# Where the second layer's norm is applied, and where its Gram products are issued: a two-layer trunk of gated attention and RWKV-7 in fp32

## The chip, the core and the metric

The kernel runs on one core of one Trainium2 chip. The metric is the device time of one execution in microseconds. Five engines work beside each other, each through its own queue in order: TensorE (PE, its weight loads shown as PEld), VectorE (DVE), ScalarE (ACT), GpSimd (POOL) and SyncE (SP, which issues DMAs).

## What is computed

T = 512 tokens of D = 2048 channels go through two residual layers. The first is a gated differential attention with 8 heads, the second a gated RWKV-7 time mixing with 32 heads of 64 channels. Each layer is `x + W_out(mixer(RMSNorm(x)) * silu(gate))`. What the change touches is the second layer's start:

```
h = rms_norm(x, gain)                       # x * rsqrt(mean(x*x) + eps) * gain, per token
p = h @ w_in                                # r, k, v, g (2048 columns each), dw, da (96 each)
p = p + (token_shift(p) - p) * mu           # token_shift: the row of the token before, zero for the first
r, k, v, g, dw, da = split(p)
w_log = -softplus(-(w0 + tanh(dw) @ decay_up)) - 0.5
a = sigmoid(a0 + da @ iclr_up)
...
S = S * w_t + sa * b_t + v_t * k_t          # a 64 x 64 state per head, token after token
y = S @ r_t
```

After this come a group norm over each head, a bonus term, the gate and the output projection with the residual.

## The kernel before, in words

**Number format.** All matmuls of the projections work on fp32 numbers split into a high and a low fp32r part. One product is three matmuls, high x high, high x low, low x high (`mm3`, L106, matmul on L108). Weights come by DMA from SP's queue (`load_w`, L78); `split_w` makes the high part wh on ACT (L96) and the low part wl on DVE (L97), with two buffers of each. The input h is kept transposed, channels on partitions, as 16 tiles hH and 16 tiles hL of 128 x 512 (`make_h`, L561: ACT writes hH on L567, DVE writes hL on L568, both from a PSUM tile that the transposes of PE filled).

**Layer 0** runs its eight heads one after the other. A head's attention is a `Chain`: a generator whose steps are issued by `tick` (L139) behind a set number of the next head's projection matmuls, so that PE's order is written out by hand. Its output projection goes over four blocks of 512 columns (loop `cb`, L537). For each, 192 matmuls fill four PSUM tiles (one per 128 tokens, number t), DVE adds the residual input (L549), ACT stores the sum x1 to memory (L550) and sums its squares into ssx (L552); then PE transposes the 16 squares of 128 x 128 (L556), four into one PSUM tile, and `make_h` writes the tiles of h with the gain but without the norm.

**The passage.** Layer 1 opens its own pools, sets its masks (POOL), sums ssx (L1009), takes the reciprocal root on DVE (`rsqrt`, L63 to L70, integer start and three Newton steps), spreads each token's factor over 128 columns (`rep`, L1016), transposes it (L1017) and copies it to `rb` (L1019): a 128 x 512 tile that holds every token's factor on every partition. The first projection is the pair dw, da ("dwda": two times 96 columns, 96 matmuls). `unit_chan` runs a group of four channel blocks for dw, then the same four for da.

**Mixing.** `shift_mix` takes a projection from PSUM. DVE multiplies it by rb into `pmix`, which has a zero column in front (L606); ACT scales it by 1 - mu (L607); DVE adds mu times the same tile shifted by one token (L608).

**Layer 1's pairs.** Sixteen pairs of heads, j = 0 to 15, each with 128 channels: projections k, r, v (48 matmuls each), and from j = 3 on also the gate of pair j - 3. Behind k comes `stage1` (decay, the tiles AR and BK; AR's first half on L724, its sums' split on L579), behind r comes `stage2`: AR's second half (L744), the Gram products gp on PE (32 products of 64 or 128 columns, L755), their masking into G on DVE (L762), and stores that hand them to `t_solve`. `t_solve` (L790) inverts the triangular matrices on DVE with 62 small operations (L810, L812) and stores Tm to memory (td, L814). `t_combine` (L820) reads it back as TT (DMAs on SP, L826), transposes on DVE (T, L834), and multiplies with G on PE twice (px, L840 and L847). `scan_pair` (L905) then carries the state over eight chunks of 64 tokens, three small products each (L916, L927, L934) with copies on ACT (L919, L929), state updates on DVE (VS, L938/L941) and copies on POOL (SA, L922). `outputs` issues the products Y (L956, and with SA on L960), `centre` takes the mean off (L971 to L973: s, yc). The steps of t_combine, scan_pair and outputs of pair j - 1 form the chain that `tick` issues behind the matmuls of pair j, at set distances (GAP_D = 18, GAP_X = 27, GAP_T = 8, then 5 or 4 matmuls).

**What sets the order.** Each engine's queue is filled at build time by a list scheduler that works from priorities (`high_priority`, with the offsets AHEAD, SCAN and SOLVE) and from anchors (`issue_after`: not before a given matmul in PE's order). On the chip each queue runs in that order.

Of the kernel before, what the change touches and what calls it, by code (L numbers as in the profile page):

```python
# [13 lines left out]
F32 = mybir.dt.float32  # L14
# [3 lines left out]
AF = mybir.ActivationFunctionType  # L18
ALU = mybir.AluOpType
AX = mybir.AxisListType  # L20
# [3 lines left out]
P = 128  # L24
D = 2048
T = 512
KT = D // P
NT = T // P
NH = 8
EPS = 1e-6  # L30
# [8 lines left out]
AHEAD, SCAN, SOLVE = 2000, 3000, 4000  # L39
# [74 lines left out]
class Chain:  # L114
# [23 lines left out]

def tick(g, m, at):  # L139

    if g.chains:
# [157 lines left out]
def head_vg(g, h, vg):  # L299

    nc, w = g.nc, g.work
    V = w.tile([P, NT, 256], F32R, name="V", tag="V", bufs=1)
    VL = w.tile([P, NT, 256], F32R, name="VL", tag="VL", bufs=1)
    G = w.tile([P, NT, 256], F32, name="G", tag="G", bufs=2)
# [12 lines left out]

def attention(g, h, qkT, qkL, sq, V, VL, G, gap, rows=None):


    nc, w = g.nc, g.work
    yT = w.tile([P, 2, T], F32, name="yTh", tag="yTh", bufs=2)
    blocks = [Ctx() for _ in range(NT)]

    def scores(t):
# [105 lines left out]
def layer0(g, aps):  # L431
# [71 lines left out]
    with ExitStack() as cx:  # L503
# [29 lines left out]

        yH, yL = Rows(rows, 0), Rows(rows, 1)
        g.ssx = g.const.tile([P, NT, 4], F32, name="ssx")
        g.hH, g.hL = [], []
        for cb in range(4):  # L537
            cs = slice(cb * 512, (cb + 1) * 512)
            pts = unit_tok(g, yH, yL, [(aps["da_w_out"][0], cb * 512, 512)], 512, more=all_rows)
            if cb < 2:  # L540
                xq = g.work.tile([P, NT, 512], F32, name="xq", tag="qkT", bufs=2)
                xs = [xq[:, t, :] for t in range(NT)]
            else:
                tags, nb = (("t1",), 4) if cb == 2 else (("p0", "p1"), 2)
                xs = [g.work.tile([P, 512], F32, name="xr", tag=tags[t % len(tags)], bufs=nb)[:] for t in range(NT)]
            for t in range(NT):
                xr = xs[t]
                nc.sync.dma_start(out=xr, in_=aps["x"][0, t * P : (t + 1) * P, cs])
                nc.vector.tensor_add(xr, xr, pts[t][:])  # L549
                nc.scalar.dma_start(out=g.xd[t * P : (t + 1) * P, cs], in_=xr)  # L550
                junk = g.work.tile([P, 512], F32, name="junkx", tag="a", bufs=2)
                nc.scalar.activation(junk[:], xr, AF.Square, accum_out=g.ssx[:, t, cb : cb + 1])  # L552
            for k in range(4):
                ps = g.ps.tile([P, 512], F32, name="pt", tag="pb")
                for t in range(NT):
                    nc.tensor.transpose(ps[:, t * P : (t + 1) * P], xs[t][:, k * P : (k + 1) * P], g.ident[:])  # L556
                make_h(g, ps, KT + cb * 4 + k)
    lx.close()


def make_h(g, ps, col):  # L561

    nc = g.nc
    hh = g.hp.tile([P, T], F32R, name="hH", tag="hH")
    hl = g.hp.tile([P, T], F32R, name="hL", tag="hL")
    w = g.prm_a[:, col : col + 1]
    m = nc.scalar.activation(hh[:], ps[:], AF.Copy, scale=w)  # L567
    nc.vector.scalar_tensor_tensor(hl[:], ps[:], w, hh[:].bitcast(F32), ALU.mult, ALU.subtract)  # L568
    g.hH.append(hh)
    g.hL.append(hl)  # L570
    return m.ins
# [8 lines left out]
    return hh, hl  # L580


def unit_chan(g, parts, cols, step=P):

    nc = g.nc
    n = cols // step
    pts = [g.pp.tile([P, 512], F32, name="pp", tag="pp") for _ in range(n)]
    KG = 8 if cols == P else 4
    for k0 in range(0, KT, KG):
        wh, wl = split_w(g, parts, KG, cols, k0)  # L590
        for c in range(n):
            s = slice(c * step, (c + 1) * step)
            for k in range(KG):
                kk = k0 + k
                mm3(nc, pts[c][:step, :], wh[:, k, s], wl[:, k, s], g.hH[kk][:], g.hL[kk][:],
                    kk == 0, kk == KT - 1, g, 3 * kk)
    return pts


@urgent  # L600
def shift_mix(g, ps, rows, mu, omu, tag, bufs=2):

    nc, w = g.nc, g.work
    p_ = g.pmix
    o_ = w.tile([P, T], F32, name="mix" + tag, tag=tag, bufs=bufs)
    nc.vector.tensor_mul(p_[:rows, 1:], ps[:rows, :], g.rb[:rows, :])  # L606
    nc.scalar.activation(o_[:rows, :], p_[:rows, 1:], AF.Copy, scale=omu)  # L607
    nc.vector.scalar_tensor_tensor(o_[:rows, :], p_[:rows, 0:T], mu, o_[:rows, :], ALU.mult, ALU.add)  # L608
    return o_


C = 64
# [3 lines left out]
RK = 96  # L616
# [30 lines left out]
def rwkv_masks(g):  # L647
# [8 lines left out]
    for lo in (0, C):  # L656
# [5 lines left out]
    g.pmix = c.tile([P, T + 1], F32, name="pmix")  # L662
    nc.gpsimd.memset(g.pmix[:, 0:1], 0.0)
# [73 lines left out]
    return p  # L737


def stage2(g, j, r, p, before):  # L740

    nc, w, BK = g.nc, g.work, p.BK
    col = lambda n: g.prm[n][:, j : j + 1]
    nc.vector.tensor_mul(p.AR[:, :, 1, :], r[:].rearrange("p (c t) -> p c t", c=NC_), p.E[:, :, 1:])  # L744
    nc.vector.scalar_tensor_tensor(r[:], r[:], col("hrk"), p.f[:], ALU.mult, ALU.mult)
    p.rf = r
    p.G = w.tile([P, NC_, 2, 2, C], F32, name="G1", tag="G1", bufs=2)
    p.BKT = w.tile([P, NC_, P], F32, name="BKT", tag="BKT", bufs=2)
    halves = []
# [64 lines left out]
    nc.sync.dma_start(out=g.td[j % 2].rearrange("q l t -> l q t"), in_=Tm[:])  # L814


GAP_D, GAP_X, GAP_T = 18, 27, 8


def t_combine(g, j, p):  # L820
# [20 lines left out]
                             start=True, stop=True, tile_position=(b0, b0 + HALF))  # L841
    for _, _, _, hi in blocks:
        nc.scalar.copy(X[hi], px[hi, :N].rearrange("p (c s) -> p c s", c=NC_))
    yield GAP_X, None
    for h, b0, lo, hi in blocks:
        for c in range(NC_):
# [1 line left out]
                             start=True, stop=True, tile_position=(b0 + HALF, b0))  # L848
    for h, b0, lo, _ in blocks:
        nc.scalar.copy(TT[lo, :, h, HALF:C], px[lo, N:].rearrange("p (c s) -> p c s", c=NC_))  # L850
        r_ = slice(b0, b0 + C)
        nc.scalar.copy(p.G[r_, :, 0, h, :], p.AR[r_, :, 0, :])
    yield GAP_T, "ACT"


# [143 lines left out]
def layer1(g, aps):  # L999
    nc, tc = g.nc, g.tc  # L1000
    with ExitStack() as cx:
# [2 lines left out]
        rwkv_masks(g)  # L1004
        w = g.work
        win = aps["rw_w_in"][0]

        ss = g.small.tile([P, NT], F32, name="ss1", tag="ss1", bufs=1)
        nc.vector.reduce_sum(ss[:], g.ssx[:], AX.X)  # L1009
        nc.vector.tensor_scalar(ss[:], ss[:], 1.0 / D, EPS, ALU.mult, ALU.add)  # L1010
        rs = g.small.tile([P, NT], F32, name="rs1", tag="rs1", bufs=1)
        rsqrt(g, rs[:], ss[:], NT, "r4")
        ps = g.ps.tile([P, 512], F32, name="pt", tag="pb", bufs=2)
        for t in range(NT):
            rep = w.tile([P, P], F32, name="rep", tag="X", bufs=1)
            nc.vector.tensor_copy(rep[:], rs[:, t : t + 1].to_broadcast([P, P]))  # L1016
            nc.tensor.transpose(ps[:, t * P : (t + 1) * P], rep[:], g.ident[:])  # L1017
        g.rb = g.lc.tile([P, T], F32, name="rb")
        nc.vector.tensor_copy(g.rb[:], ps[:])  # L1019
        pts = unit_chan(g, [(win, 4 * D, 2 * RK)], 2 * RK, RK)  # L1020
        g.dwda = []
        for i in range(2):
            m = shift_mix(g, pts[i], RK, g.mut[:, i : i + 1], g.omut[:, i : i + 1], "r")
            if i == 0:
                nc.scalar.activation(m[:RK, :], m[:RK, :], AF.Tanh)
            g.dwda.append(split_act(g, m[:RK, :], g.lc, f"dd{i}"))
        pairs = []
        for j in range(D // P):
            c0 = j * P
# [5 lines left out]
            def proj(i, j=j):  # L1035
                return unit_chan(g, [(win, i * D + j * P, P)], P)[0]
# [4 lines left out]
            if j:  # L1041
# [87 lines left out]
```

## Time and profile before

| | |
|---|---|
| median of 3 runs | 2238.08 us (2234.47 to 2239.84) |
| the profiled execution | 2246.47 us, of it 2244.7 us from the first to the last instruction |
| mean granted TensorE clock | 0.996 |
| instructions | 33817 |
| ACT busy | 957.4 us (43%) |
| POOL busy | 249.2 us (11%) |

In the profile PE, PEld, DVE, ACT, POOL and SP are the engines, L12 is line 12 of the kernel, and names are those of the program's tiles. A row of a timeline has the start (us), the duration (us), the engine, the line, the operation, `out<-in`, the matmul's size, the output's shape and how many such records stand together; in square brackets is the idle time of the engine just before, and what ended it. Matmuls overlap each other, so a row's duration is longer than the distance to the next start; where a stream runs without stalls that distance is what counts. A row of a group has the count behind an x, then the total busy time in us and the mean of one in ns, then the idle time before and what ended it. The granted clock is 1.00 at full speed.

Layer 0 and its output projection end at about 1001 us, the pairs run from 1030 to about 2060 us, the rest is the last pair's chain and the second output projection.

### The profile page before, as it was taken

How to read it: one execution, taken by the hardware profiler on the slowest of the kernel's cores; microseconds unless marked ns; L12 is line 12 of the kernel's file. 1: busy time of each engine (PE TensorE's matmuls, PEld its weight loads, DVE VectorE, ACT ScalarE, POOL GpSimd, SP SyncE). 2: the span in 40 equal slices, each digit the busy share in tenths (PEclk: the TensorE clock that was granted, in tenths of full speed). 3: DMA queues.
4: the chain of work that ended last, by engine and by line, in shares of the span. 5: the costliest groups of instructions: out<-in, count | busy, mean ns of one | idle time of the engine just before them, and what ended most of it. 6: DMA issues, size and time to landing. Idle time of an engine off the chain costs nothing.

```text
span 2244.7 us, 33817 instructions
## 1 busy us (share of the span) xinstructions
PE 2194.9 (98%) x12264; PEld 1776.1 (79%) x12264; DVE 1447.7 (64%) x3825; ACT 957.4 (43%) x1969; POOL 249.2 (11%) x613
## 2 busy tenths in 40 slices
PE   8999999999999999999999999999999999999999
PEld 6888888888888878877777777777777777777887
DVE  5555646455564663345778888888888888876322
ACT  5443434344343452233345555545445545545211
POOL 0000000000000000001122222222222222222000
PEclk9999999999999999999989999999999999999999
DMA  6222222232223263333412333333333333334343
GB/s 179 94 86 95 85 94 94 85 95 83 95 85 103 85 203 125 123 95 94 108 49 71 91 88 89 87 98 89 86 90 82 88 86 94 95 102 132 132 131 113
DMA packets 290730, 224.46 MB, mean 100 GB/s; under 512 B 47732, under 2 KB 255748, under 8 KB 290564
## 3 DMA queue, kind: packets, MB, share of 16 engines
q1 hardware_dynamic: 275892, 195.74, 30.1%
q0 software_dynamic: 6144, 10.84, 1.9%
q10 hardware_dynamic: 8528, 15.73, 1.9%
q8 instruction: 96, 1.57, 0.3%
q14 instruction: 70, 0.57, 0.1%
HBM read 202.26 MB, written 19.99 MB: 99 GB/s over the span
## 4 chain that ended last, share of the span: by engine, by line
PE 59%; DVE 27%; DMA 6%; issue 5%; ACT 3%; SPq 0%; POOL 0%; DVEq 0%; ACTq 0%; POOLq 0%
PE pp L108 46%; DVE wl L97 5%; DVE tmpl L810 4%; PE pt L108 4%; DVE Tm L812 3%; DMA TT<-td 2%; DVE VS L938 2%; DMA td<-Tm 1%; DMA ltd<-ssl 1%; ACT wh L96 1%; PE gp L755 1%; PE sc L108 1%; DVE t L269 1%; PE Y L956 1%; DVE mixv L608 1%
## 5 line engine op out<-in xcount | busy, mean ns | idle before, releaser
L97 DVE TENSOR_TENSOR wl<-wraw,wh 128x1024 fp32r<-128x1024 f32 (+2 forms) x325 | 394.6, 1214 | 467.4 <-ACT wh L96 467.2
L96 ACT CAST wh<-wraw 128x1024 fp32r<-128x1024 f32 (+2 forms) x325 | 340.0, 1046 | 636.1 <-PE pp L108 446.3
L108 PE MATMUL pp<-wh,hH 128*128 128x512 f32 x1408 | 555.1, 394 | 6.4 <-ACT hH L567 5.3
L108 PE MATMUL pp<-wh,hL 128*128 128x512 f32 x1408 | 552.8, 393 | 1.1 <-DVE hL L568 0.6
L108 PE MATMUL pp<-wl,hH 128*128 128x512 f32 x1408 | 553.0, 393 | 0.0
L108 PE MATMUL pp<-hL,wh 128*128 128x512 f32 (+1 forms) x1056 | 429.0, 406 | 0.0
L108 PE MATMUL pp<-hH,wh 128*128 128x512 f32 (+1 forms) x1056 | 426.4, 404 | 0.0
L108 PE MATMUL pp<-hH,wl 128*128 128x512 f32 (+1 forms) x1056 | 425.2, 403 | 0.0
L108 PEld LDWEIGHTS pp<-wh,hH 128*128 128x128 f32 x1408 | 265.0, 188 | 61.2 <-ACT hH L567 6.1
L108 PEld LDWEIGHTS pp<-wh,hL 128*128 128x128 f32 x1408 | 265.0, 188 | 55.8 <-DVE hL L568 1.3
L108 PEld LDWEIGHTS pp<-wl,hH 128*128 128x128 f32 x1408 | 265.1, 188 | 52.1
L108 PEld LDWEIGHTS pp<-hH,wh 128*128 128x128 f32 (+1 forms) x1056 | 198.8, 188 | 37.0 <-issue 0.2
L108 PEld LDWEIGHTS pp<-hL,wh 128*128 128x128 f32 (+1 forms) x1056 | 199.1, 189 | 36.1 <-issue 1.7
L108 PEld LDWEIGHTS pp<-hH,wl 128*128 128x128 f32 (+1 forms) x1056 | 199.0, 188 | 35.6 <-issue 0.2
L810 DVE SCALAR_TENSOR_TENSOR tmpl<-LT,Tm 128x60 f32<-128x60 f32 (+24 forms) x496 | 134.2, 270 | 10.7
L803 POOL MEMSET Tm<- 128x256 f32 x16 | 5.0, 316 | 1058.0 <-PE pt L556 1009.4
L922 POOL COPY SA<-VS 64x64 f32<-64x64 f32 x224 | 72.7, 325 | 443.2 <-DVE VS L938 391.1
L812 DVE TENSOR_TENSOR Tm<-Tm,tmpl 128x60 f32<-128x60 f32 (+24 forms) x496 | 102.9, 207 | 11.1
L919 ACT COPY rhs<-sm 64x64 f32<-64x64 f32 x256 | 52.7, 206 | 96.8 <-PE sm L916 94.3
L929 ACT COPY VS<-sm 64x64 f32<-64x64 f32 x256 | 52.8, 206 | 62.7 <-PE sm L927 49.7
L916 PEld LDWEIGHTS sm<-VS,G 128*128 128x128 f32 x256 | 43.9, 189 | 30.2 <-PE pp L108 16.7
L925 POOL TENSOR_SCALAR Sg<-SA,gam 128x64 f32<-128x64 f32 x96 | 66.7, 695 | 9.3
(274 smaller groups left out, 2798.6 us busy)
## 6 DMA issues: line engine op xcount, KB each, us to landing
wraw<-in_rw_w_in_dram SPq DMA_DIRECT2D x128, 512.0 KB, 4.1
wraw<-in_da_w_in_dram SPq DMA_DIRECT2D x254, 256.0 KB, 3.0
wraw<-in_da_w_out_dram SPq DMA_DIRECT2D x32, 512.0 KB, 3.7
wraw<-in_rw_w_out_dram SPq DMA_DIRECT2D x32, 512.0 KB, 3.7
LT<-ltd POOLq DMA_DIRECT2D x64, 132.0 KB, 2.9
yr<-yd SPq DMA_DIRECT2D x28, 256.0 KB, 3.7
xr<-xd SPq DMA_DIRECT2D x16, 256.0 KB, 4.5
out_dram<-xr ACTq DMA_DIRECT2D x16, 256.0 KB, 4.4
```

What stands on the lines that cost most here:

```text
L96: nc.scalar.copy(hi[:, ks], raw[:, ks])
L97: nc.vector.tensor_sub(lo[:, ks], raw[:, ks], hi[:, ks].bitcast(F32))
L108: m = nc.tensor.matmul(out, a, b, start=s, stop=e)
L269: nc.vector.tensor_add(t1[:], t1[:], t2[:])
L810: nc.vector.scalar_tensor_tensor(tt, LT[:, i : i + 1, i + 1 :].to_broadcast([P, s, n]), n2[:, i : i + 1], Tm[:, 0:s, i : i + 1].to_broadca ...
L812: nc.vector.tensor_add(Tm[:, 0:s, i + 1 :], Tm[:, 0:s, i + 1 :], tt)
L916: nc.tensor.matmul(sm[:, 0:P], both(p.G[:, c, 0]), both(VS[:, c]), start=True, stop=True)
L919: nc.scalar.copy(rhs[r_, :], sm[r_, h * C : h * C + C])
L922: nc.gpsimd.tensor_copy(p.SA[r_, c - 1, :], VS[r_, c, h, :])
L925: nc.gpsimd.tensor_scalar(Sg[:], p.SA[:, c - 1, :], p.gam[:, c : c + 1], None, ALU.mult)
L929: nc.scalar.copy(VS[r_, c, h, :], sm[r_, P : P + C])
L938: nc.vector.scalar_tensor_tensor(VS[r_, c + 1, h, :], s_, p.gam[r_, c : c + 1], Sg[r_, :], ALU.mult, ALU.add)
```

## The change

It has three parts.

1. **The norm is applied before the transposes.** The four column blocks of x1 stay in four tiles xq. The loop over column blocks has no transposes and no `make_h` any more. Behind the loop the reciprocal root is taken in two parts, for token blocks 0 to 2 and for block 3. A new function `more_h` multiplies each row block of xq by its tokens' factors (a 128 x 512 tensor_scalar on DVE, 16 of them), transposes (PE) and calls `make_h`. It is called inside the dwda projection, which has moved into layer 0's pools; that projection now runs dw and da for each channel block in turn, and asks for the blocks of h two ahead.

2. **Mixing straight from PSUM.** rb, rep, pmix and the multiplication on L606 go. ACT scales the PSUM tile by 1 - mu, DVE adds mu times the PSUM tile shifted by one token, on columns 1 to 511.

3. **The Gram products.** `stage2` keeps AR's second half; the products, their masking and the stores are a function `gram`, called with `t_solve` and `group_norm` behind the 15th matmul of the v projection instead of ahead of it. `t_combine` copies AR's first half to G before its second set of products, GAP_X is 19, and what `finish` issues is anchored behind the last matmul. G and yTh of layer 0 have one buffer instead of two.

The core of the diff:

```diff
@@ Chain.finish, tick
         while self.wait is not None:
-            self.step(g)
+            with g.tc.issue_after(g.m.ins):
+                self.step(g)
@@ end of layer 0
-            for k in range(4):
-                ps = g.ps.tile([P, 512], F32, name="pt", tag="pb")
-                for t in range(NT):
-                    nc.tensor.transpose(ps[:, t * P : (t + 1) * P], xs[t][:, k * P : (k + 1) * P], g.ident[:])
-                make_h(g, ps, KT + cb * 4 + k)
+        for a, b in ((0, NT - 1), (NT - 1, NT)):
+            nc.vector.reduce_sum(ss[:, a:b], g.ssx[:, a:b, :], AX.X)
+            nc.vector.tensor_scalar(ss[:, a:b], ss[:, a:b], 1.0 / D, EPS, ALU.mult, ALU.add)
+            rsqrt(g, rs[:, a:b], ss[:, a:b], b - a, f"r{b - a}")
+
+        def more_h(n, m):
+            for k in range(len(g.hH), min(n, KT)):
+                xq, c0 = xs[k // 4], k % 4 * P
+                ps = g.ps.tile([P, 512], F32, name="xT", tag="pa", bufs=2)
+                for t in range(NT):
+                    if c0 == 0:
+                        with tc.high_priority(offset=AHEAD):
+                            nc.vector.tensor_scalar(xq[:, t, :], xq[:, t, :], rs[:, t : t + 1], None, ALU.mult)
+                    with tc.issue_after(m.ins) if m else ExitStack():
+                        nc.tensor.transpose(ps[:, t * P : (t + 1) * P], xq[:, t, c0 : c0 + P], g.ident[:])
+                with tc.high_priority(offset=AHEAD):
+                    make_h(g, ps, KT + k)
+
+        pts = unit_chan(g, [(aps["rw_w_in"][0], 4 * D, 2 * RK)], 2 * RK, RK, more_h)
+        g.dwda = []
+        for i in range(2):
+            m = shift_mix(g, pts[i], RK, g.mut[:, i : i + 1], g.omut[:, i : i + 1], "t1", 4)
...
@@ unit_chan
-        for c in range(n):
+        for k, c in [(k, c) for k in range(KG) for c in range(n)]:
             s = slice(c * step, (c + 1) * step)
-            for k in range(KG):
...
+            if more and c == 0:
+                more(kk + 2, m)
+            m = mm3(nc, pts[c][:step, :], wh[:, k, s], wl[:, k, s], g.hH[kk][:], g.hL[kk][:],
                     kk == 0, kk == KT - 1, g, 3 * kk)
+            if n == 1 and 3 * kk + 3 == behind[0]:
+                behind[1](m)
@@ shift_mix
-    nc.vector.tensor_mul(p_[:rows, 1:], ps[:rows, :], g.rb[:rows, :])
-    nc.scalar.activation(o_[:rows, :], p_[:rows, 1:], AF.Copy, scale=omu)
-    nc.vector.scalar_tensor_tensor(o_[:rows, :], p_[:rows, 0:T], mu, o_[:rows, :], ALU.mult, ALU.add)
+    nc.scalar.activation(o_[:rows, :], ps[:rows, :], AF.Copy, scale=omu)
+    nc.vector.scalar_tensor_tensor(o_[:rows, 1:], ps[:rows, 0 : T - 1], mu, o_[:rows, 1:], ALU.mult, ALU.add)
@@ t_combine
-GAP_D, GAP_X, GAP_T = 18, 27, 8
+GAP_D, GAP_X, GAP_T = 18, 19, 8
...
+    for h, b0, _, _ in blocks:
+        r_ = slice(b0, b0 + C)
+        nc.scalar.copy(p.G[r_, :, 0, h, :], p.AR[r_, :, 0, :])
     yield GAP_X, None
@@ layer1
-            stage2(g, j, r, p, j and pairs[j - 1].chain)
-            t_solve(g, j, p)
-            if j > 1:
-                group_norm(g, j - 2, pairs[j - 2])
-            vps = proj(2)
+            stage2(g, j, r, p)
+
+            def behind(m, j=j, p=p):
+                with tc.issue_after(m.ins):
+                    gram(g, j, p, j and pairs[j - 1].chain)
+                t_solve(g, j, p)
+                if j > 1:
+                    group_norm(g, j - 2, pairs[j - 2])
+
+            vps = proj(2, behind=(15, behind))
```

The lines of layer 1 that made rb, and the dwda projection there, go.

More of the change, by code (lines that the diff above doesn't have):

```diff
@@ L139, in tick @@
 def tick(g, m, at):
+    g.m = m
     if g.chains:
@@ L303, in head_vg @@
     VL = w.tile([P, NT, 256], F32R, name="VL", tag="VL", bufs=1)
-    G = w.tile([P, NT, 256], F32, name="G", tag="G", bufs=2)
+    G = w.tile([P, NT, 256], F32, name="G", tag="G", bufs=1)
     for t in range(NT):
@@ L321, in attention @@
     nc, w = g.nc, g.work
-    yT = w.tile([P, 2, T], F32, name="yTh", tag="yTh", bufs=2)
+    yT = w.tile([P, 2, T], F32, name="yTh", tag="yTh", bufs=1)
     blocks = [Ctx() for _ in range(NT)]
@@ L535, in layer0 @@
         g.ssx = g.const.tile([P, NT, 4], F32, name="ssx")
-        g.hH, g.hL = [], []
+        g.hH, g.hL, xs = [], [], []
         for cb in range(4):
@@ L539, in layer0 @@
             pts = unit_tok(g, yH, yL, [(aps["da_w_out"][0], cb * 512, 512)], 512, more=all_rows)
[L540 to L545, printed above, removed]
+            xq = g.work.tile([P, NT, 512], F32, name="xq", tag=("qkT", "qkL")[cb // 2], bufs=2)
+            xs.append(xq)
             for t in range(NT):
-                xr = xs[t]
+                xr = xq[:, t, :]
                 nc.sync.dma_start(out=xr, in_=aps["x"][0, t * P : (t + 1) * P, cs])
@@ L552, in layer0 @@
                 nc.scalar.activation(junk[:], xr, AF.Square, accum_out=g.ssx[:, t, cb : cb + 1])
-            for k in range(4):
-                ps = g.ps.tile([P, 512], F32, name="pt", tag="pb")
-                for t in range(NT):
-                    nc.tensor.transpose(ps[:, t * P : (t + 1) * P], xs[t][:, k * P : (k + 1) * P], g.ident[:])
-                make_h(g, ps, KT + cb * 4 + k)
+        rs = g.small.tile([P, NT], F32, name="rs1", tag="rs1", bufs=1)
+        ss = g.small.tile([P, NT], F32, name="ss1", tag="ss1", bufs=1)
+        for a, b in ((0, NT - 1), (NT - 1, NT)):
[6 more added lines that the diff above has]
+                ps = g.ps.tile([P, 512], F32, name="xT", tag="pa", bufs=2)
+                for t in range(NT):
+                    if c0 == 0:
[9 more added lines that the diff above has]
+            m = shift_mix(g, pts[i], RK, g.mut[:, i : i + 1], g.omut[:, i : i + 1], "t1", 4)
+            if i == 0:
+                nc.scalar.activation(m[:RK, :], m[:RK, :], AF.Tanh)
+            g.dwda.append(split_act(g, m[:RK, :], g.const, f"dd{i}"))
     lx.close()
@@ L580, in split_act, with unit_chan @@
     return hh, hl
-def unit_chan(g, parts, cols, step=P):
+def unit_chan(g, parts, cols, step=P, more=None, behind=(0, None)):
     nc = g.nc
@@ L661, in rwkv_masks @@
                                 base=0, pattern=[[1, C]], channel_multiplier=-1)
-    g.pmix = c.tile([P, T + 1], F32, name="pmix")
-    nc.gpsimd.memset(g.pmix[:, 0:1], 0.0)
     g.hdec = c.tile([P, 1], F32, name="hdec")
@@ L737, in stage1, with stage2 @@
     return p
-def stage2(g, j, r, p, before):
-    nc, w, BK = g.nc, g.work, p.BK
+def stage2(g, j, r, p):
+    nc = g.nc
     col = lambda n: g.prm[n][:, j : j + 1]
@@ L746, in stage2, with gram @@
     p.rf = r
+def gram(g, j, p, before):
+    nc, w, BK = g.nc, g.work, p.BK
     p.G = w.tile([P, NC_, 2, 2, C], F32, name="G1", tag="G1", bufs=2)
@@ L850, in t_combine @@
         nc.scalar.copy(TT[lo, :, h, HALF:C], px[lo, N:].rearrange("p (c s) -> p c s", c=NC_))
-        r_ = slice(b0, b0 + C)
-        nc.scalar.copy(p.G[r_, :, 0, h, :], p.AR[r_, :, 0, :])
     yield GAP_T, "ACT"
@@ L1006, in layer1 @@
         win = aps["rw_w_in"][0]
[L1008 to L1013, printed above, removed]
-        for t in range(NT):
[L1015 to L1026, printed above, removed]
         pairs = []
@@ L1033, in layer1, with proj @@
             up = split_act(g, u[:], w, "up")
-            def proj(i, j=j):
-                return unit_chan(g, [(win, i * D + j * P, P)], P)[0]
+            def proj(i, j=j, **k):
+                return unit_chan(g, [(win, i * D + j * P, P)], P, **k)[0]
             p = stage1(g, j, shift_mix(g, proj(1), P, *mus(g, 1, j), "k"), up)
```

5 lines of the change are left out of this document (2 added, 3 removed).

## The prediction

> **What bounds the kernel now.** I read the page's busy shares first, then the windows around the passage between the layers, then the timelines of those windows.
>
> ```profile
> PE 2194.9 (98%) x12264; PEld 1776.1 (79%) x12264; DVE 1447.7 (64%) x3825; ACT 957.4 (43%) x1969; POOL 249.2 (11%) x613
> ...
> 994.61 0.39 PE L108 MATMUL pp<-wl,hH 128*128 128x512 f32 x1
> ...
> 996.43 0.39 PE L108 MATMUL pp<-wh,hH 128*128 128x512 f32 x1
> ...
> 1000.00:1030.00 30.00, 27.55 (x122) 19.10 (x122) 13.84 (x32) 9.06 (x17) 3.85 (x20) 0.94 0.39 117
> ...
> 1726.00:1789.00 63.00, 61.10 (x422) 49.39 (x424) 52.62 (x142) 31.64 (x72) 15.32 (x37) 1.00 0.34 89
> ```
>
> TensorE is the bound. The two matmuls are eight starts apart: (996.43 - 994.61)/8 = 0.2275 us for each 512-column matmul. Their number doesn't change, so a gain can only come out of PE's stalls, and every new PE stall is paid in full. VectorE is busy 52.62 of 63 us in a late pair's window: not the bound, but full enough to be late. (A window's row: length, then busy time and instructions of PE, PEld, DVE, ACT and POOL, granted clock, DMA share, GB/s.) Three places have stalls or a low granted clock: the passage between the layers (0.94 in its window), the first pairs, and the Gram products of every pair. I price the change place by place.
>
> **1. The passage from out-projection to k0.** Before:
>
> ```profile
> 1000.96 0.39 PE L108 MATMUL pp<-wh,hL 128*128 128x512 f32 x1
> ...
> 1006.45 0.60 PE L556 MATMUL pt<-ident,xr 128*128 128x128 f32 x4
> 1006.80 0.48 PE L108 MATMUL pp<-hH,wh 128*96 128x512 f32 x1
> ...
> 1016.65 0.30 PE L1017 MATMUL pt<-ident,rep 128*128 128x128 f32 x1 [2.00 <-issue]
> ...
> 1030.12 0.39 PE L108 MATMUL pp<-hH,wh 128*128 128x512 f32 x1
> ...
> 1001.39 0.69 DVE L549 TENSOR_TENSOR xr<-xr,pp 128x512 f32<-128x512 f32 x1 [0.68 <-PE pp L108]
> 1002.30 0.96 DVE L97 TENSOR_TENSOR wl<-wraw,wh 128x768 fp32r<-128x768 f32 x1 [0.22 <-ACT wh L96]
> 1003.54 0.17 DVE L1009 TENSOR_REDUCE ss<-ssx 128x4 f32<-128x16 f32 x1 [0.28 <-ACT junkx L552]
> ...
> 1006.45 0.16 DVE L70 SCALAR_TENSOR_TENSOR rs<-rs_t,rs_i 128x4 f32<-128x4 f32 x1
> ```
>
> The last out-projection matmul starts at 1000.96, k0's first at 1030.12: 29.16 us, nearly all of it dwda matmuls, because before needs no norm before it multiplies. The reduce and rsqrt run beside them on DVE. After, the whole norm stands ahead of the first dwda matmul. DVE's issue order is: adds, wl, the reduce for blocks 0 to 2 with its rsqrt (mixed with part of block 3's), twelve normalisations in a row, seven last small steps of block 3's rsqrt, four normalisations. PE has nothing else in its queue.
>
> ```profile
> L198 DVE TENSOR_SCALAR nturn<-ang 128x256 f32<-128x256 f32 x1 | 0.3, 285 | 0.0
> ...
> L636 DVE TENSOR_SCALAR omu<-prmin_rw_mu_dram 128x64 f32<-128x64 f32 x1 | 0.2, 185 | 0.0
> ...
> L606 DVE TENSOR_TENSOR pmix<-pp,rb 128x512 f32<-128x512 f32 x64 | 44.0, 688 | 15.0 <-PE pp L108 13.7
> ...
> L567 ACT ACTIVATE hH<-pt,prmin_norm_w_dram 128x512 fp32r<-128x512 f32 x16 | 11.0, 688 | 26.5 <-PE pp L108 19.8 <-PE pt L556 6.7
> ...
> L568 DVE SCALAR_TENSOR_TENSOR hL<-pt,prmin_norm_w_dram,hH 128x512 fp32r<-128x512 f32 x16 | 12.0, 748 | 22.2 <-ACT hH L567 22.2
> ...
> L607 ACT ACTIVATE mixr<-pmix,omut 96x512 f32<-96x512 f32 x2 | 1.4, 720 | 2.7 <-DVE pmix L606 2.7
> ...
> L608 DVE SCALAR_TENSOR_TENSOR mixr<-pmix,mut,mixr 96x512 f32<-96x512 f32 x2 | 1.5, 746 | 0.9 <-ACT mixr L607 0.9
> ...
> 1783.48 0.44 DVE L834 STREAM_TRANSPOSE T<-TT 64x256 f32<-64x256 f32 x1 [0.56 <-DMA TT<-td]
> 1783.85 0.38 DVE L973 TENSOR_TENSOR yc<-Y,s 128x256 f32<-128x256 f32 x1
> ```
>
> A 128x512 tensor_scalar isn't in the trace. From 64 to 256 columns the time goes from 185 to 285 ns, 0.52 ns a column, so 285 + 256 x 0.52 = 418 ns at 512. Neighbours in a full DVE queue overlap: the one at 1783.48 takes 0.44 and the next starts 0.37 later. I take 0.35 us each; the ceiling is L606's 0.69.
>
> Clock from the last out-projection matmul: add starts +0.43; wl ends +2.30; reduce +2.35; rsqrt (2.9 us from 1003.54 to 1006.45 for one chain) ready near +5.0; twelve normalisations 4.2, +9.2; seven small steps at 0.2, +10.6; first of the last four, +11.0; transposes 0.35 (1006.45 to 1006.80), +11.4; hH 0.69, first matmul near +12.1; hL 0.75, so the stream runs from +13. Then 94 matmuls, 21.4, and the 14 other transpose groups, 4.9: +39.3. k0's first matmul now waits until both mixes have read dwda's PSUM: 0.4 + 0.72 + 0.65 + 0.75, less one pitch, 2.3: +41.6. Gone are the 2.00 us hole and the rep transposes, both inside the 29.16.
>
> The clock adds to it:
>
> ```profile
> 1017.80:1021.20 3.40, 3.40 (x11) 2.33 (x10) 1.76 (x4) 0.00 (x0) 0.00 (x0) 0.51 0.32 73
> ...
> 1120.20:1133.90 13.70, 13.70 (x81) 10.44 (x80) 4.63 (x13) 7.57 (x17) 0.23 (x1) 0.50 0.15 44
> ...
> 1119.10 0.69 PE L840 MATMUL px<-T,G 32*32 32x32 f32 x16 [2.27 <-DVE T L834]
> ```
>
> Idle times of 2.00 and 2.27 us were each followed by a stretch at clock 0.51 and 0.50, 3.4 and 13.7 us long; half of each is lost, 1.7 and 6.8. An idle time of 11 us will surely bring one: I take the short one, 1.7 (ends 0 and 6.8; the old 1.7 goes with its hole, already inside 29.16). The passage is 43.3 us. Twelve transpose groups, 12 x 0.35 = 4.2, leave the out-projection. Net: 43.3 - 29.16 - 4.2 = **+9.9 us** (ends +6, if DVE's small steps pack better and no slow spell comes, and +19, at 0.69 a normalisation (13 x 0.34 = 4.4) and the long spell (5.1)).
>
> [...]
>
> **2. The first pairs.** px of pair 0 moves from behind k2's 41st matmul to behind its 30th, and waits for the same solve. It waited 2.27; 11 x 0.2275 = 2.5 more if the solve comes no sooner; four mixes of pair 0 to 2 without L606 give back a little: **+2.2** (0 to +2.5). The Gram products of pair 1 come later in v1, behind 18 matmuls, and their wait mostly goes: **-0.9**.
>
> Then the Y products. Before they are spread in fours; after, chain 0 and 1 issue twelve, then twos, as late pairs issue sixteen:
>
> ```profile
> 1149.86 0.49 PE L934 MATMUL sm<-VS,BKT 128*128 128x128 f32 x2
> 1150.28 0.45 PE L956 MATMUL Y<-VS,G 128*64 128x64 f32 x4
> 1150.65 0.50 PE L108 MATMUL pp<-hH,wh 128*128 128x512 f32 x1
> ...
> 1779.44 1.20 PE L956 MATMUL Y<-VS,G 128*64 128x64 f32 x32
> 1780.57 0.68 PE L960 MATMUL Y<-SA,AR 64*64 64x64 f32 x28
> ```
>
> Thirty-two records in one go take 1780.57 - 1779.44 = 1.13 us. Eight groups of four take 8 x 0.37 (1150.28 to 1150.65) = 2.96, and the two records ahead of each hold PE for 0.42 (1149.86 to 1150.28), about 0.2 more than without the switch: 2.96 - 1.13 + 8 x 0.2 = 3.4 us a chain. Twelve of sixteen together save three quarters, 2.5. Two chains: -5. Chain 2's scan steps also stand five matmuls apart in place of two to four, about -1. Together **-6** (0, if px of pairs 1 and 2, now 28 and 45 matmuls sooner, stall by 2 to 3 us each, to -10).
>
> **3. The late pairs.** Sixty-six multiplications of L606 go, 0.69 us each, 45 us of DVE. PE doesn't wait for them as such; what counts is AR:
>
> ```profile
> PE gp L755 <- DVE AR L744: 8.8, 12, 1.3
> ...
> PE sm L916 <- DVE VS L938: 7.4, 20, 0.6
> ...
> 1781.44 0.75 DVE L971 TENSOR_REDUCE s<-Y 128x4 f32<-128x256 f32 x2
> ...
> 1782.18 0.74 DVE L724 SCALAR_TENSOR_TENSOR AR<-mixk,prm_nkk,E 128x512 f32<-128x512 f32 x1
> ...
> 1784.22 0.67 DVE L606 TENSOR_TENSOR pmix<-pp,rb 128x512 f32<-128x512 f32 x1
> 1785.40 0.44 DVE L834 STREAM_TRANSPOSE T<-TT 64x256 f32<-64x256 f32 x1 [0.51 <-DMA TT<-td]
> ...
> 1786.22 1.22 DVE L97 TENSOR_TENSOR wl<-wraw,wh 128x1024 fp32r<-128x1024 f32 x1
> ...
> 1788.13 0.69 DVE L744 TENSOR_TENSOR AR<-mixr,E 128x512 f32<-128x512 f32 x1
> ```
>
> (A wait's row: total us, times, longest.) The Gram products stall 8.8 us over 12 pairs, 0.73 each. The multiplication at 1784.22 lies between two transposes that wait for a transfer: without it the second waits 0.67 longer for the same landing at 1785.40, and AR is no earlier. And the Gram products do not land behind the 15th matmul: in the order issued they stand behind the 20th of v in a late pair (19th before). Y and SA now precede v's first matmul (1.9 us), so from r's end the slack is 1.9 + 20 x 0.2275 = 6.4 us; in it DVE must do wl 1.22 (which waits for ACT's half, 1.2 as I estimate), two T 0.9, sums and their scaling 1.05, the mix 0.75, two centrings 0.75, and both ARs 0.74 and 0.69: 7.3. A wait of 0.9 in place of 0.73: **0** (ends -0.73 and +0.7 a pair, eleven pairs: -8 to +8).
>
> **4. The tail.** Chain 14 has its Y products together (twelve and twos), chain 15 partly: **-1.5** (-3 to +1).
>
> Sum: 9.9 + 2.2 - 0.9 - 6 + 0 - 1.5 = **+3.7 us**. The profiled execution took 2246.47 us (span 2244.7 and 1.77 around it) and would take 2250.2. The median of the runs is 2238.08, 8.4 less; I carry the difference over: **2241.8 us**. A measurement of this kernel can tell about 0.2%, 4.5 us, from no change.
>
> **Rivals.**
> A, faster: the Gram wait goes. Place: DVE's queue ahead of AR. If the lighter DVE ends the solve sooner, td and TT land 1 us or more earlier, T doesn't wait, and AR meets PE. It decides at 6.4 us behind r's end. For it: DVE loses 2.1 us a pair, and the T waits of 0.56 and 0.51 are DMA's. Against: the solve's 62 steps are paced by a chain of their own. Price 11 x -0.73 = -8, and half of the 7.4 us for which scan steps wait on DVE, -3.5: 2241.8 - 11.5 = 2230.
>
> B, slower: the passage at its upper end, 0.69 us a normalisation and the long half-clock spell, +9: 2251.
>
> [...]
>
> That the Gram part does not do what it says is in the forecast at zero.
>
> **How the numbers follow.** Forecast 0.36, its own range 2237 to 2248 (0.22 of it slower by over 0.2%, 0.14 within). A 0.27 (0.23 faster, 0.04 within), B 0.25, all slower. C 0.12 (0.03 faster, 0.09 within). Faster 0.26, within 0.27, slower 0.47. The range 2229 to 2257 reaches from A's time to B with a Gram wait of 0.5 more a pair (+6). The cheap ends of the other parts in A's case lie below it, the dear ones in B's above, 1 in 10 each.
>
> **What would show it.** Last out-projection matmul to k0's first: near 43 us, with an idle PE of 10 to 11 us and a normalisation of 0.42. Below 36 or above 50 my passage is wrong. The wait of px of pair 0 over 4 us. Gram waits of 0.6 to 1.2 in late pairs; if they are 0, A holds. Y of chain 0 in one group of twelve. Late pairs still 62 to 64 us apart; a shift of 0.5 us there outweighs everything but the passage.

## The result and the profile after

The changed kernel takes 2254.15 us (median of 4 runs, 2253.53 to 2258.59), the kernel before 2238.95 in the same comparison: a ratio of 1.0076, 95% interval 1.0057 to 1.0095. The forecast was 2241.8, slower, in a range of 2229 to 2257. The direction and the range held; the loss is 15 us where 3.7 were worked out.

One thing first, because all that follows leans on it. The first profile of the kernel before shows an execution of 2246.5 us, 8 over its median. Run e12 below is a second profile of the same kernel, at 2237.45, and is what the changed kernel's profile (2254.08) is compared with here. "Layer 0" ends with the last out-projection matmul, the passage with k0's first; gp0 is the first start of the Gram products, and so on. The half-clock column is half the length of the spells of half clock between gp0 and gp5: 13.65, 10.24 and 3.41 us long by the trace's record of the granted clock.

| kernel, profiled execution | layer 0 | passage | k0 to gp0 | gp0 to gp5 | of it lost at half clock | mean of ten late pairs | gp15 to the end |
|---|---|---|---|---|---|---|---|
| before, first profile, 2246.5 | 1001.0 | 29.2 | 26.9 | 291.5 | 6.8 | 62.85 | 267.6 |
| before, second profile, 2237.5 | 1000.0 | 29.2 | 26.9 | 288.6 | 5.1 | 62.33 | 267.6 |
| changed, 2254.1 | 994.0 | 46.0 | 27.0 | 283.7 | 1.7 | 63.54 | 266.3 |
| changed less second before | -6.0 | +16.8 | +0.1 | -4.9 | -3.4 | +1.21 | -1.3 |

The sum is -6.0 + 16.8 + 0.1 - 4.9 + 12.1 - 1.3 = +16.8 with the rounded terms, and the two executions differ by 16.6.

The two profiles of the kernel before differ by 0.52 us a late pair, so it matters which one is ordinary. Each run's span times its mean granted clock estimates its time at full clock (the clock is recorded to 0.001, 2.2 us, so a single run is good to about 1 us). The second profile has 2229.0 us and the mean of its ten runs is 2229.1; the first has 2235.7.

The passage, PE's timeline of the changed kernel:

```profile
994.03 0.39 PE L108 MATMUL pp<-wh,hL 128*128 128x512 f32 x1
999.44 1.64 PE L568 MATMUL xT<-ident,xq 128*128 128x128 f32 x6 [5.02 <-DVE xq L566]
1005.46 0.69 PE L568 MATMUL xT<-ident,xq 128*128 128x128 f32 x2 [4.39 <-DVE xq L566]
1006.71 0.74 PE L108 MATMUL pp<-hH,wh 128*96 128x512 f32 x1 [0.56 <-ACT hH L588]
...
1037.88 0.40 PE L108 MATMUL pp<-hH,wl 128*96 128x512 f32 x1
1040.01 0.51 PE L108 MATMUL pp<-hH,wh 128*128 128x512 f32 x1 [1.74 <-DVE mixt L631]
```

PE stands twice, 5.02 and 4.39 us, each time until a normalisation is done; the first dwda matmul starts 12.7 us behind the last one of layer 0. DVE's timeline shows what the two waits are made of:

```profile
998.61 0.16 DVE L70 SCALAR_TENSOR_TENSOR rs<-rs_t,rs_i 128x3 f32<-128x3 f32 x1
998.69 0.15 DVE L68 SCALAR_TENSOR_TENSOR rs_t<-rs_t,ss 128x1 f32<-128x1 f32 x1
998.80 4.84 DVE L566 TENSOR_SCALAR xq<-xq,rs 128x512 f32<-128x512 f32 x12
1003.56 0.15 DVE L70 SCALAR_TENSOR_TENSOR rs_i<-rs_t,rs_i 128x1 f32<-128x1 f32 x1
...
1004.91 1.67 DVE L566 TENSOR_SCALAR xq<-xq,rs 128x512 f32<-128x512 f32 x4
```

Twelve normalisations take 1003.56 - 998.80 = 4.76 us, 0.40 each, and the last four can only follow block 3's rest.

The late pairs, PE's waits over ten of them, first the kernel before (second profile), then the changed one (total us, times, longest):

```profile
PE sm L916 <- DVE VS L938: 5.3, 15, 0.4
PE gp L755 <- DVE AR L744: 4.2, 7, 1.3
PE sm L927 <- ACT rhs L919: 2.0, 10, 0.2
PE sm L934 <- ACT VS L929: 0.3, 2, 0.2
```

```profile
PE sm L943 <- DVE VS L965: 21.8, 30, 1.0
PE sm L943 <- DVE VS L968: 3.6, 5, 1.1
```

The Gram wait is gone, as rival A had it. In its place PE waits for the scan's state updates on DVE: 25.4 us in all where every wait together was 11.8. That is 13.6 us more, against the 12.1 by which the ten pairs grew. And DVE has less to do, the windows of the ten pairs say, again before and then after (length; PE, PEld, DVE, ACT, POOL busy; clock; DMA share; GB/s):

```profile
1344.80:1968.10 623.30, 609.74 (x4203) 493.32 (x4202) 524.97 (x1411) 317.28 (x720) 153.16 (x370) 1.00 0.34 91
```

```profile
1350.60:1986.10 635.50, 608.75 (x4202) 494.27 (x4202) 505.81 (x1372) 314.63 (x719) 137.16 (x370) 1.00 0.33 89
```

DVE's work falls by 19.2 us over ten pairs, and PE's waits for DVE rise from 9.5 to 25.4. One of these waits, in the changed kernel: the product that feeds the update starts at 1777.72, and the next product of the chain waits 0.97 us until 1780.65.

```profile
1777.72 0.38 PE L961 MATMUL sm<-VS,BKT 128*128 128x128 f32 x2
...
1780.65 0.46 PE L943 MATMUL sm<-VS,G 128*128 128x128 f32 x2 [0.97 <-DVE VS L965]
```

```profile
1777.00 1.22 DVE L731 TENSOR_TENSOR_SCAN l<-rmask,th 128x512 f32<-128x512 bf16 x1
1778.14 0.16 DVE L838 TENSOR_TENSOR Tm<-Tm,tmpl 128x24 f32<-128x24 f32 x1
1778.26 0.17 DVE L734 TENSOR_SCALAR m<-l 128x8 f32<-128x8 f32 x1
1778.34 0.69 DVE L748 SCALAR_TENSOR_TENSOR th<-th,mixk 128x512 f32<-128x512 f32 x1
1778.94 0.23 DVE L836 SCALAR_TENSOR_TENSOR tmpl<-LT,Tm 128x16 f32<-128x16 f32 x1
1779.09 0.69 DVE L736 TENSOR_TENSOR l<-l,m 128x512 f32<-128x512 f32 x1
1779.69 0.17 DVE L838 TENSOR_TENSOR Tm<-Tm,tmpl 128x16 f32<-128x16 f32 x1
1779.78 0.27 DVE L965 SCALAR_TENSOR_TENSOR VS<-sm,gam,Sg 64x64 f32<-64x64 f32 x1
1779.97 0.21 DVE L836 SCALAR_TENSOR_TENSOR tmpl<-LT,Tm 128x8 f32<-128x8 f32 x1
1780.22 0.29 DVE L965 SCALAR_TENSOR_TENSOR VS<-sm,gam,Sg 64x64 f32<-64x64 f32 x1
```

The update is one operation for each of the pair's two heads. The first starts 2.06 us behind the product, since the queue holds stage 1 of the next pair and the tail of the solve ahead of it; a step of the solve stands between the two as well, and PE goes on when the second is done.

### The profile page after: what moved, and what is told of

Read it like the earlier page. It is cut to its first block, busy times and chain, and to the rows that moved or that the text cites. A ratio compares the mean times of both kernels' runs of the same rounds, so it can differ in the third digit from the quotient of the medians.

```text
span 2252.3 us, 33774 instructions
## 1 busy us (share of the span) xinstructions
PE 2178.0 (97%) x12260; PEld 1770.4 (79%) x12260; DVE 1422.2 (63%) x3783; ACT 955.2 (42%) x1969; POOL 228.8 (10%) x612
## 5 line engine op out<-in xcount | busy, mean ns | idle before, releaser
L836 DVE SCALAR_TENSOR_TENSOR tmpl<-LT,Tm 128x60 f32<-128x60 f32 (+24 forms) x496 | 133.9, 270 | 12.2
L838 DVE TENSOR_TENSOR Tm<-Tm,tmpl 128x60 f32<-128x60 f32 (+24 forms) x496 | 104.8, 211 | 12.7
L949 POOL COPY SA<-VS 64x64 f32<-64x64 f32 x224 | 60.1, 268 | 476.2 <-DVE VS L965 390.6
L943 PE MATMUL sm<-VS,G 128*128 128x128 f32 x256 | 55.2, 297 | 32.6 <-DVE VS L965 27.0
```

The lines of the kernel that those rows point to most:

```text
L836: nc.vector.scalar_tensor_tensor(tt, LT[:, i : i + 1, i + 1 :].to_broadcast([P, s, n]), n2[:, i : i + 1], Tm[:, 0:s, i : i + 1].to_broadca ...
L838: nc.vector.tensor_add(Tm[:, 0:s, i + 1 :], Tm[:, 0:s, i + 1 :], tt)
L943: nc.tensor.matmul(sm[:, 0:P], both(p.G[:, c, 0]), both(VS[:, c]), start=True, stop=True)
L949: nc.gpsimd.tensor_copy(p.SA[r_, c - 1, :], VS[r_, c, h, :])
```

## The experiments

The theory after the result: the passage costs what the forecast said, and the late pairs lose because part 3 puts the scan's updates behind other DVE work (theory A). The rival: they lose because part 2's shorter mix shifts DVE's order (theory B). Late-pair means below stand against 62.33 (second profile of before) and 63.54 (changed).

**e1, part 3 undone.**

```diff
-            stage2(g, j, r, p)
-            ...
-            vps = proj(2, behind=(15, behind))
+            stage2(g, j, r, p)
+            gram(g, j, p, j and pairs[j - 1].chain)
+            t_solve(g, j, p)
+            ...
+            vps = proj(2)
...
-GAP_D, GAP_X, GAP_T = 18, 19, 8
+GAP_D, GAP_X, GAP_T = 18, 27, 8
...
```

> Parts 1 and 2 of the change, part 3 undone (Gram products, solve and group norm ahead of the v projection, GAP_X 27, the copies of AR and finish as before). Theory A (the late pairs lose because part 3 puts the scan's state updates behind solve and stage-1 work in DVE's queue): the period of the late pairs goes from 63.5 back to 62.9 us, PE's waits for the state updates (VS) fall from 32 to 8 us, the Gram products wait again 0.7 us a pair, and the time is about 11 x 0.65 = 7 us under the changed kernel's, 2247. Theory B (the late pairs lose because the mix without its multiplication reorders DVE's queue): period 63.5, time 2254. By both the passage stays at 46 us.

Measured: 2254.84 us, ratio 1.0075 (1.0062 to 1.0088), so no gain in the median. Passage 46.2. Nine of the ten late pairs take 62.8 to 63.0, one 64.58. Against 62.33 that is still 0.5 a pair, and PE's waits say of what:

```profile
PE sm L959 <- ACT VS L954: 15.9, 21, 1.2
PE sm L941 <- DVE VS L963: 7.9, 10, 0.8
PE gp L780 <- DVE AR L764: 0.3, 1, 0.3
```

Now the scan waits for ACT's copies, and the Gram products don't wait again (0.3 us in all, where 0.7 a pair was expected). So parts 1 and 2 alone cost the late pairs something too, and through the scan again; theory A is not the whole.

**e2, part 3 alone in the kernel before.** The same edit the other way round, with the norm and the mix of before.

> Part 3 alone in the kernel before (norm and mixing as before). Theory A: the late pairs' period is 63.5 us, the waits for VS some 25 to 30 us, and the time 2238.5 + 7 = 2245 to 2246, less 1 to 2 for the first pairs and the tail. Theory B: period 62.9 or less, time 2236 to 2239. By both the passage is 29 us.

Measured: 2241.31, ratio 1.0017 (1.0008 to 1.0026); late pairs 62.98; passage 29.2.

```profile
PE sm L926 <- DVE VS L948: 13.6, 30, 0.7
PE sm L926 <- DVE VS L951: 4.0, 5, 1.0
PE gp L764 <- DVE AR L748: 1.1, 2, 0.9
```

Part 3 takes the Gram wait away (4.2 to 1.1) and brings 17.6 us of waits for the updates (5.3 before): 0.65 us a pair lost in this profile. The time of theory A, 2245 to 2246, didn't come: the median is 3.5 us over the kernel before, partly because the first pairs were 1.9 us faster at full clock.

**e3, the multiplication back** (64 of them, by one).

```diff
-    nc.scalar.activation(o_[:rows, :], ps[:rows, :], AF.Copy, scale=omu)
-    nc.vector.scalar_tensor_tensor(o_[:rows, 1:], ps[:rows, 0 : T - 1], mu, o_[:rows, 1:], ALU.mult, ALU.add)
...
+    nc.vector.tensor_mul(p_[:rows, 1:], ps[:rows, :], g.rb[:rows, :].to_broadcast([rows, T]))
+    nc.scalar.activation(o_[:rows, :], p_[:rows, 1:], AF.Copy, scale=omu)
+    nc.vector.scalar_tensor_tensor(o_[:rows, :], p_[:rows, 0:T], mu, o_[:rows, :], ALU.mult, ALU.add)
...
```

> The changed kernel with the multiplication back in the mix of k, r, v and g, by one in place of the norm's factor: 64 times 0.69 us of DVE work that part 2 took away (the products by one change no number). Theory A: DVE has less room, the period stays at 63.5 or rises by up to 1 us, time 2254 to 2264. Theory B: the order of before comes back, period 62.9, time 2247.

Measured: 2252.0, ratio 1.0064 (1.0051 to 1.0078); late pairs 62.90, updates waited for 16.0 us. With 44 us of DVE work put back the late pairs are 0.64 us faster each, and what is left is e2's loss. Its first pairs lost 6.8 us at half clock where the changed kernel lost 1.7, which is why the time hardly shows it. With e1 and e2: parts 1 and 2 without part 3 cost the late pairs 0.5 to 0.7 us each, part 3 alone 0.65, all 1.21. Each theory had about half of it, as far as one profile of each can tell.

**e4, one reciprocal root**, so that the first column block's normalisations come first.

```diff
-        for a, b in ((0, NT - 1), (NT - 1, NT)):
+        for a, b in ((0, NT),):
```

> The changed kernel with the reciprocal root taken once for all four token blocks, so that the four normalisations of the first column block come first and nothing stands between. If the passage's idle PE is the wait for DVE's queue of twelve normalisations and seven small steps: the first dwda matmul starts near +8 us after the last out-projection matmul in place of +12.7, the passage is 41 in place of 46 us, time 2249 to 2250. If something else ends last (the weights, the clock), it stays within 1 us of 2254.

The passage did as the first case says, 41.3 us, with one wait in place of two:

```profile
1001.44 2.06 PE L568 MATMUL xT<-ident,xq 128*128 128x128 f32 x8 [5.40 <-DVE xq L566]
1003.85 0.74 PE L108 MATMUL pp<-hH,wh 128*96 128x512 f32 x1 [0.35 <-ACT hH L588]
```

The time did not: 2255.49, ratio 1.0079 (1.0065 to 1.0093). The stages of its profile against the changed kernel's: passage -4.7, layer 0 +1.6 (a spell of 3.4 us at half clock near 817), gp0 to gp5 +6.5 (6.8 more at half clock, 8.5 against 1.7), late pairs -1.1, end -1.0. The spell behind the first px lasted 3.4 us in the changed kernel and 13.7 here (and one more of 3.4 came at 1179):

```profile
1124.20:1137.90 13.70, 12.95 (x87) 9.93 (x88) 5.46 (x18) 3.51 (x10) 0.00 (x0) 0.51 0.14 39
```

**e5 and e6, part 3 split.** e5 keeps the place of the Gram products and undoes the rest in t_combine:

```diff
-GAP_D, GAP_X, GAP_T = 18, 19, 8
+GAP_D, GAP_X, GAP_T = 18, 27, 8
...
-        nc.scalar.copy(p.G[r_, :, 0, h, :], p.AR[r_, :, 0, :])
     yield GAP_X, None
...
+        nc.scalar.copy(p.G[r_, :, 0, h, :], p.AR[r_, :, 0, :])
```

> The changed kernel with t_combine's order as before (copies of AR behind the second products, GAP_X 27); the Gram products still behind the 15th v matmul. Undoing part 3 alone, or part 2 alone, brought the late pairs back to 62.9 to 63.0 us, so the loss of 0.65 us a pair needs both. If it needs the place of the Gram products: period 63.4 to 63.6, waits for VS over 20 us, time 2253 to 2255. If it needs the earlier copies and the shorter GAP_X: period 62.9, waits for VS under 12 us, time 2247.

e6 undoes the place (the first half of e1's diff) and keeps the rest.

> The reverse: Gram products, solve and group norm ahead of the v projection as before, but the copies of AR early and GAP_X 19. If the loss needs the place: period 62.9 and waits for VS under 12 us. If it needs GAP_X and the copies: period 63.4 or more. Time 2247 to 2250 in the first case, 2253 to 2255 in the second.

Measured: e5 2253.38, ratio 1.0073 (1.0054 to 1.0091), late pairs 63.03 (one of 64.64, the others 62.7 to 63.4), waits for the updates 13.7. e6 2255.80, ratio 1.0079 (1.0065 to 1.0093), late pairs 63.32, waits 19.1 for DVE's updates and 5.9 for ACT's copies. So undoing the early copies and the short GAP_X gives back 0.5 us a pair, as much as undoing all of part 3 (e1), and undoing the place alone 0.2. Both lost 6.8 us at half clock in the first pairs, and neither time falls.

Two things limit this reading. The list scheduler moves more than the edit names: counted in PE's order, the Gram products of a late pair stand behind the 19th v matmul before, the 20th in the changed kernel and e2, the 18th in e5 and the 16th in e1 and e6, so none of these edits restores the old place. And the half clock hides the gains in every run, not only in the profiled ones. By span times (1 - mean clock), the changed kernel's runs lost 9.6 us on average, and those of e1, e3, e5 and e6 between 12.2 and 15.4. At full clock, by the same estimate, they stand under the changed kernel's 2243.7: e1 by 4.8, e3 by 5.8, e5 by 7.4 and e6 by 3.5 us, against 5.0, 6.4, 5.1 and 2.2 gained in the ten late pairs of their profiles.

**e7, later steps.** Three more matmuls behind the updates of chunks 4, 5 and 6. (In the order issued, the Gram products of a late pair then stand behind the 16th v matmul and not the 20th.)

```diff
-        yield gap_s, "ACT"
+        yield gap_s + (3 if 4 <= c <= 6 and gap == 5 else 0), "ACT"
```

> The changed kernel with three more matmuls (0.7 us) behind the state updates of chunks 4, 5 and 6, where PE waits 0.7, 1.0 and 0.5 us for VS in every late pair. If those waits are the late pairs' loss, they go: waits for VS from 26 to under 10 us, period 62.8 to 63.0, time 2247 to 2248. If DVE's backlog moves along, the period stays at 63.4 or more and the Gram products begin to wait.

Measured: 2249.23, ratio 1.0051 (1.0036 to 1.0066), 5 us under the changed kernel though its first pairs lost 6.8 us at half clock. Late pairs 62.85:

```profile
PE sm L954 <- ACT rhs L946: 10.7, 20, 1.1
PE sm L943 <- DVE VS L968: 1.4, 1, 1.4
```

The waits for the updates fall from 25.4 to 1.4, and a part comes back as waits for ACT's rhs copies. The edit takes no work from DVE; it only lets PE ask later, and gives back 0.69 of the 1.21 us. So more than half of the late pairs' loss is the distance between the chain's steps and the engines' queues. A wait that goes doesn't come back in full: over the ten pairs the waits fall by 13.3 us, PE's busy time grows from 608.8 to 616.0, and the pairs gain 6.9. Why it grows stays open. The Gram products' place moved along, but with the same place e1 and e6 have 63.04 and 63.32.

**e8, the first px later** (in the kernel before: ten matmuls, 2.3 us).

```diff
-    if before:
+    if before and j > 1:
...
-    yield GAP_D, None
+    yield GAP_D if j else 99, None
```

> The kernel before with the first chain's px held back to the third matmul of r2, ten matmuls (2.3 us) later, the length of its wait for T; what follows in that chain moves along. If that wait is what brings the half-clock spell near 1120 us: no wait over 1 us there and no spell, 64 us from the second to the third Gram products without it, time 2234 to 2236 with little spread. If spells come by themselves, one appears elsewhere and the time stays at 2238 with the same spread of 6 us.

Measured: 2242.09, ratio 1.0020 (1.0007 to 1.0032), with a wider spread, 2236 to 2247. The wait and the spell near 1120 are gone, but a spell of 10.2 us stands at 1239 (5.1 us lost), and gp1 to gp2 takes 71.2 us at full clock, with 429 PE records in it in place of 397: as the chain comes later, more of it falls there. The spell wasn't the property of that one wait.

**e9 and e10: a version under the kernel before?** e9 is e2 with e7's edit, e10 the kernel before with two matmuls more behind the updates of chunks 1 and 3.

> Part 3 alone in the kernel before, with the three more matmuls behind the state updates of chunks 4, 5 and 6. Part 3 alone had late pairs of 62.98 us with 17.6 us of waits for VS over ten pairs and 2.2 us of Gram waits, against 62.85, 6.8 and 9.5 before. If the later steps take its waits away as in the changed kernel (0.69 us a pair): period 62.2 to 62.4, and the time 2241.3 less 5 to 7 us, 2234 to 2236, under the kernel before. If the Gram products wait in their place: 62.9 and 2240.

> The kernel before with two more matmuls behind the state updates of chunks 1 and 3, where PE waits 0.3 and 0.4 us for VS in a late pair. If a wait for VS costs what it lasts: 62.85 less 0.5 to 0.7 a pair, time 2238 less 3 to 6. If the Gram products, which wait 0.7 us for AR, take it up: unchanged, 2238.

Measured: e9 2237.92, ratio 1.0006 (0.9996 to 1.0015), late pairs 62.77, with 11.3 us of waits for rhs copies in place of the updates. e10 2238.52, ratio 1.0003 (0.9993 to 1.0012), late pairs 62.43, waits for the updates 4.3 (5.3 before) and for AR 5.3 (4.2). Neither can be told from the kernel before. For e9 that is a miss of both cases; for e10 it is the second case, unchanged, though the waits as a whole fell by 2.2 us and PE's busy time grew by 3.3, as in e7. I had set the expectations against the first profile's 62.85; against 62.33 there was less to gain.

**e11, e4 and e7 together.**

> The changed kernel with one reciprocal root (passage 41 in place of 46 us) and the later steps (period 62.85 in place of 63.54). Each had its own stage shorter; the first did not show in the time, for its half-clock spell behind the first px cost 6.6 us in place of 1.9. If stage savings add: 2249.2 - 4 = 2245, still 7 over the kernel before, the passage's rest. If the passage's saving is always given back: 2249.

Measured: 2247.35, ratio 1.0047 (1.0035 to 1.0059), 1.9 us under e7. Its passage is 40.3 where e7's is 45.0, layer 0 1.3 longer, the half clock in the first pairs the same 6.8. In the profiles 2.9 of the passage's 4.6 us arrive, in the medians 1.9 where 4 were expected. So a stage's saving isn't always given back, nor does all of it arrive. It still stands 10.6 us over the kernel before (2236.73 in this comparison), with a passage that is 40.3 - 29.2 = 11.1 us longer.

**e12, the kernel before again.**

> The kernel before once more, unchanged, for a second profile of it. Its first profiled execution took 2246.5 us, 8 to 9 over the median of its runs, and had a half-clock spell of 13.7 us behind the first px that cost 6.8. If that spell belongs to that one execution: 63 to 66 us from the second to the third Gram products in place of 71.2, and a profiled execution within 4 us of 2238. If it belongs to the kernel: 71 us again, and 2245 or so.

Measured: 2237.63, ratio 1.0009 (0.9999 to 1.0020), profiled execution 2237.45. gp1 to gp2 took 69.2 us with a spell of 10.2 us. So a spell there was in both profiles, three quarters as long here; but late pairs took 62.33 in place of 62.85. The first profile was longer for another reason than I had thought: 5.2 of its 9 us are in the late pairs.

## Why the prediction was right in direction and wrong in size

**The passage: right.** Forecast 43.3 us, less 4.2 in layer 0, net +9.9. Measured 46.0 and -6.0, net +10.8. The terms that were off cancel: a group of four transposes inside a stream costs (49.1 - 43.5) / 11 = 0.5 us and not 0.35, since the matmul behind it starts late too (both profiles have 192 matmuls in the last column block, 49.1 us with eleven groups before and 43.5 with none after; in e12 a group starts at 957.50, the matmul behind it at 957.86 and the next one at 958.17, 0.31 later where a pitch is 0.23). That made the out-projection's gain larger and the dwda stretch longer. The first matmul came at +12.7 (forecast +12.1), and half of the 5.3 us at half clock behind it, 2.7, was lost where 1.7 was put. k0 started 2.13 us behind the last dwda matmul, 1.9 more than a pitch (forecast 2.3).

**The first pairs: right in sum, not in parts.** Forecast 2.2 - 0.9 - 6 = -4.7, measured -4.9. But 3.4 of it is a shorter half-clock spell, the Gram wait of pair 1 stayed (1.16 us, 1.06 before), and px waited 3.13 where before had 2.27 and 1.79 (the sign was "over 4 us"). The work itself gained 1.5 us, not 4.7. With px 1.3 later and the Gram wait no shorter, some 3 us are left for the Y products where 6 were put; no run takes them apart. That the sum came out is luck. The Y products do stand together, and the spell behind px did shrink to 3.4 us, from 10.2 in the second profile and 13.7 in the first.

**The late pairs: wrong.** The step that failed is "A wait of 0.9 in place of 0.73: **0** (ends -0.73 and +0.7 a pair, eleven pairs: -8 to +8)". It priced the Gram wait and nothing else. The Gram wait went from 0.42 to 0, the good end, and the pairs still lost 1.21 us each, beyond the bad end, at another wait of the same engine. In the prediction the scan's waits stand only in rival A, as a gain of half of 7.4 us "for which scan steps wait on DVE"; over ten pairs they went from 5.3 to 25.4. A lighter engine was taken to be an earlier one. By the prediction's own sign, Gram waits of 0, A held; but the sign told of one wait only. Its last line had the better one: a shift of 0.5 us a pair outweighs everything but the passage. e7 shows that the waits are more than half of the loss; e2, e1 and e3 show that both edits bring them. That the exact order of DVE's and ACT's queues against the scan's steps sets them is what the timelines show in single cases; why the scheduler put each operation there wasn't tried.

**The tail: right**, -1.3 for -1.5.

**Rivals.** A's mechanism came with the opposite sum. B's time of 2251 lies nearest to the measured one, but by luck: the passage was dearer than forecast by 0.9 us net and not by 9. A normalisation took 0.40 us, and the half clock, 13.7 us from 998.3 to 1012.0, lay for 8.4 us ahead of the first dwda matmul. The upper end of the range, 2257, was made of B and a longer Gram wait; that it held the measured time, which came from the scan's waits, is luck too. The 0.12 on C stood for a shorter spell behind px. It came, but what sets a spell's length stays open, and the late pairs' 12.1 us outweighed it.

**Carrying the profile over.** I took 8.4 us off the sum as if they lay evenly. e12 shows where they lay: 5.2 in the late pairs, 1.7 in the spell and 1.2 in the rest of the first pairs, 0.9 in layer 0. The Gram wait that I offered as a gain of 0.73 a pair was 0.42 in the second profile.

## What to carry to other kernels

When work is taken off an engine that feeds the bound, or a step is anchored elsewhere, price all waits of the bounding engine on that queue, not only the one the edit aims at: here one wait of 0.4 us a pair went and three of 0.5 to 1.0 us came. And don't count a wait that goes at its full length: in e7 about half of it arrived. A norm that stood beside the matmuls and now stands ahead of them costs its whole chain, and that could be read off the profile: to within 1 us net, with the passage 2.7 and layer 0 1.8 us off the other way. Before a sum is made against one profiled execution, see whether it is an ordinary one; a second profile of the same kernel is worth more than another decimal.

## What the runs showed of the hardware

The half-clock spells don't follow the length of the idle time before them. After 1.33 us idle ahead of a later px (e2) 13.7 us; 1.74 ahead of k0 (changed) none; 1.79 ahead of the first px (e12) 10.2; 2.00 on L1017 (before, first profile) 3.4; 2.27 ahead of the first px (the same) 13.7; 3.13 ahead of the first px (changed) 3.4.

In the changed kernel the spell of 3.4 us came behind this wait:

```profile
1127.62 0.77 PE L866 MATMUL px<-T,G 32*32 32x32 f32 x16 [3.13 <-DVE T L860]
```

```profile
1128.30:1131.70 3.40, 3.40 (x21) 2.34 (x20) 2.93 (x11) 0.62 (x1) 0.00 (x0) 0.53 0.53 149
```

In e2 the one of 13.7 us came behind the idle time of 1.33 us, and PE was busy through all of it:

```profile
1230.14 0.43 PE L849 MATMUL px<-T,G 32*32 32x32 f32 x8 [1.33 <-DVE T L843]
```

```profile
1231.90:1245.60 13.70, 13.70 (x79) 10.37 (x78) 7.53 (x25) 4.54 (x12) 0.94 (x3) 0.50 0.21 61
```

What brings a spell, and what sets its length, stays open here. With half of 3.4 to 13.7 us lost, a spell moves a stage by 2 to 7 us, as much as most of the edits here, so the stages had to be compared with the clock beside them.

A 128x512 tensor_scalar in fp32 with its scalar read from a tile starts every 0.40 us (the twelve on L566 in the changed kernel) and takes 0.48 each, against 0.35 forecast; the two-input form on L606 took 0.69 in the kernel before.
